# Input projection: two column halves in one matmul, drained by ACT and added by POOL

## The chip, the core and the metric

The kernel runs on one core of one Trainium2 chip, in one launch. The metric is device time in microseconds, the median of several executions. TensorE (PE in the profile) multiplies matrices into PSUM; VectorE (DVE), ScalarE (ACT) and GpSimd (POOL) work element by element; SyncE (SP) issues the transfers.

## The reference

Two layers over a sequence of 512 positions with 2048 features, in float32. The change concerns the first projection of the first layer alone:

```python
h = rmsnorm(x, norm_g)
proj = h @ w_in                       # 512 x 2048 times 2048 x 8192
u, gate = proj[..., :W_A], proj[..., W_A:]
u = u.reshape(B, S, N_POOL_GROUPS, G_A)
pooled = jnp.stack([causal_mean_pool(u[:, :, gi], w) - u[:, :, gi]
                    for gi, w in enumerate(POOL_WINDOWS)], axis=2)
y = jnp.einsum('bsgc,gcd->bsgd', pooled, w_group).reshape(B, S, W_A) * scale
return x + (y * jax.nn.silu(gate)) @ w_out
```

The second layer (latent attention) follows. It is not touched.

## The kernel before, in words

**High and low parts.** Every float32 operand is held as two fp32r numbers, a high part and the remainder. A product is three matmuls: high weights by high x, high weights by low x, low weights by high x.

**Seven products.** The projection's 64 output tiles (128 features by 512 positions) are computed as 32 pairs. For the last 30 pairs a 2 x 2 scheme with seven products in place of eight is used: the two output tiles of the pair, the two contraction tiles `2j`, `2j+1` and the two halves of the positions (`H` = 256 columns) form 2 x 2 blocks. `w_combos` (L300) loads 2 x 256 KB of weights for a quarter `q` of the contraction (two values of j), forms the sums of weights that the scheme needs (DVE L308, POOL L310 and L311), casts all seven to high parts (ACT L314) and subtracts for the low parts (DVE L315). Raw weights have three buffers, high and low weights two each. The sums of x are made once, ahead (`x_parts`, `x_sums`), into `xcp[j]`, a tile of 128 x (2, 7, 256): high and low, seven products, 256 columns.

**Matmuls.** `seven` (L326) is called for each j. For each of the seven products it issues three 256-column matmuls (L333, L335, L337) into one half of a PSUM bank. A pair has eight j (`NJ`), so 8 x 7 x 3 = 168 matmuls, and the text calls a quarter of it (42) a step. A pair's four banks hold the seven products; pairs alternate between two sets of four banks. Several products of the scheme go to both output tiles, so `gather` (L340) combines the products: one ACT copy of a half bank (L343), then four DVE additions that each read one input from PSUM (L344 to L347). The two results go to DRAM (L356), or, for the first four pairs of the u features (pairs 0 to 3, late in the loop), first through `pool_tile` (L235), which runs on DVE (L243, L250, L256, L259) with a small POOL memset.

**Around it.** Before the loop, four gate tiles are accumulated for all j into four banks `accs` while x is prepared (L386 to L388, with 256 and 512 columns mixed), copied out by ACT (L396) and stored. In the loop, the sum of squares of x is formed in the pairs n = 1 to 8 (`squares`: ACT L408, DVE L410), and n = 9 makes the norm from it (`norm_r`, with `rsqrt` at L156). The stages after the loop use 512-column matmuls (L144 to L146).

**Order.** The order of each engine's instructions is settled when the program is built: a list scheduler walks the traced instructions with a simulated timeline and fixes a list for every engine, and on the chip each engine works its list in order, waiting on semaphores. A tile pool with `bufs` buffers makes the writer of a buffer wait for the readers of its former content.

Of the kernel before, what the change touches and what calls it, by code (L numbers as in the profile page):

```python
# [14 lines left out]
P = 128  # L15
# [32 lines left out]
def trunk_kernel(  # L48
# [213 lines left out]
    with ExitStack() as c1:  # L262
# [4 lines left out]
        ps7 = [c1.enter_context(tc.tile_pool(name=f"ps7{i}", bufs=1, space=bass.MemoryType.PSUM, **tile_))  # L267
               for i in range(2)]
        xh, xl = [None] * NJ, [None] * NJ
# [7 lines left out]
        def x_parts(j, c, hp):  # L277
# [4 lines left out]
            xh[j], xl[j] = h, lo  # L282
# [37 lines left out]
        def banks(n):  # L320
            return [ps7[n % 2].tile([P, 2, H], F32, tag=f"k{i}", name=f"k{i}") for i in range(4)]


        SEVEN = ((2, 0, 0, 0), (0, 6, 1, 0), (1, 2, 2, 0), (3, 4, 3, 0),
                 (5, 5, 0, 1), (6, 1, 1, 1), (4, 3, 2, 1))

        def seven(ks, w, j):
            hi, lo = w
            for wi, xi, b, h in SEVEN:
                dst = ks[b][:, h, :]  # L330
                first, last = j == 0 and h == 0, j == NJ - 1

                T.matmul(dst, hi[:, j % 2, wi, :], xh[j][:, xi, :], start=first, stop=False,  # L333
                         skip_group_check=True)
                T.matmul(dst, hi[:, j % 2, wi, :], xl[j][:, xi, :], start=False, stop=False,  # L335
                         skip_group_check=True)
                T.matmul(dst, lo[:, j % 2, wi, :], xh[j][:, xi, :], start=False, stop=last,  # L337
                         skip_group_check=True)

        def gather(ks, pair):  # L340

            e = epool.tile([P, 7, H], F32, tag="e", name="e")
            A.copy(e[:, 6, :], ks[2][:, 0, :])  # L343
            V.tensor_tensor(e[:, 0:2, :], e[:, 6:7, :].broadcast_to([P, 2, H]), ks[0], ALU.add)  # L344
# [14 lines left out]
        accs = banks(1)  # L359
# [801 lines left out]
```

## Time and profile before

| what | value |
|---|---|
| median of 3 runs | 1923.71 us (1923.11 to 1924.19) |
| span of the profiled execution | 1921.5 us |
| median less span | 2.2 us |
| granted TensorE clock | 1.000 |
| input projection with seven products, first to last matmul | 52.7 to 661.4 us |
| PE, DVE, ACT, POOL busy in the whole span | 99%, 67%, 42%, 15% |

The profile shows one execution: for each engine the instructions with start and duration, grouped by line of the code and by the names of output and inputs. A bracket or the field behind the last bar gives the idle time before an instruction and who ended it. The record of a matmul lasts longer than its share of the engine, since matmuls overlap, so the pace is read from the starts. An instruction's record on DVE or POOL includes time in which it was held up after its start. Only the span of the profiled execution is known, and the 2.2 us around it come from the median.

### The profile page before, as it was taken

The page shows a single profiled execution, that of the slowest core. Times are in us where ns is not written, and L with a number is a line of the kernel's source. Part 1 is how long each engine was busy: PE and PEld are TensorE (multiplying, and loading weights), DVE is VectorE, ACT ScalarE, POOL GpSimd, SP SyncE. Part 2 cuts the span into 40 slices and gives each one's busy share as a digit, 9 for nine tenths or more (in the row PEclk, how much of TensorE's full clock was granted, in tenths as well). Part 3 has the DMA queues.
Part 4 walks back from the last instruction along what each step waited for, and adds up shares of the span by engine and source line. Part 5 has one row for each costly group of instructions (what it writes and reads, how often), then busy time and mean ns, then how long its engine had stood idle before and what let it go on. Part 6 is the DMA issues. An engine that isn't in the chain of part 4 may idle for free.

```text
span 1921.5 us, 30674 instructions
## 1 busy us (share of the span) xinstructions
PE 1906.1 (99%) x11356; PEld 1704.7 (89%) x11356; DVE 1278.6 (67%) x2252; ACT 807.1 (42%) x1509; POOL 280.9 (15%) x436
## 2 busy tenths in 40 slices
PE   8999999999999999999999999999999999999999
PEld 7999999999999988888888888888888898988887
DVE  8677785797666777496595476564325888897332
ACT  8443433333333433233333355233225777775221
POOL 0333233343222100000000000000001232320000
PEclk9999999999999999999999999999999999999999
DMA  6454444344444546344334344333333222234632
GB/s 191 155 164 157 151 132 133 121 131 135 147 146 135 159 154 214 119 128 142 119 123 137 110 146 134 89 98 120 121 121 90 87 90 69 85 124 144 203 116 88
DMA packets 177078, 251.26 MB, mean 131 GB/s; under 512 B 15776, under 2 KB 96800, under 8 KB 176928
## 3 DMA queue, kind: packets, MB, share of 16 engines
q1 hardware_dynamic: 176640, 249.10, 41.4%
q8 instruction: 89, 1.46, 0.3%
q14 instruction: 61, 0.50, 0.1%
q10 hardware_dynamic: 288, 0.20, 0.0%
HBM read 216.21 MB, written 33.03 MB: 130 GB/s over the span
## 4 chain that ended last, share of the span: by engine, by line
PE 94%; DVE 3%; DMA 1%; issue 1%; ACT 0%; SPq 0%; POOL 0%; DVEq 0%; POOLq 0%; ACTq 0%
PE mm L145 16%; PE mm L146 16%; PE mm L144 16%; PE k L337 10%; PE k L335 10%; PE k L333 10%; PE sc L786 3%; PE mm L641 2%; PE mm L643 2%; PE mm L642 2%; PE mm L664 1%; PE mm L666 1%; PE mm L665 1%; PE tr L814 1%; PE tr L752 1%; DMA raw<-awin 1%
## 5 line engine op out<-in xcount | busy, mean ns | idle before, releaser
L126 ACT CAST whi<-raw 128x512 fp32r<-128x512 f32 (+2 forms) x424 | 255.9, 607 | 518.6 <-PE mm L145 438.5
L333 PE MATMUL k<-xc,hi 128*128 128x256 f32 x1680 | 460.1, 283 | 0.0
L335 PE MATMUL k<-xc,hi 128*128 128x256 f32 x1680 | 460.0, 283 | 0.0
L127 DVE TENSOR_TENSOR wlo<-raw,whi 128x512 fp32r<-128x512 f32 (+2 forms) x424 | 285.7, 675 | 235.7 <-ACT whi L126 232.6
L337 PE MATMUL k<-xc,lo 128*128 128x256 f32 x1680 | 417.9, 283 | 2.2 <-DVE lo L315 2.2
L146 PE MATMUL mm<-bt,wlo 128*128 128x512 f32 x944 | 368.1, 390 | 0.0
L144 PE MATMUL mm<-bt,whi 128*128 128x512 f32 x944 | 367.7, 390 | 0.0
L145 PE MATMUL mm<-bt,whi 128*128 128x512 f32 x944 | 367.2, 389 | 0.0
L314 ACT CAST hi<-raw 128x1792 fp32r<-128x1792 f32 x120 | 202.8, 1690 | 364.9 <-PE k L337 249.6
L315 DVE TENSOR_TENSOR lo<-raw,hi 128x1792 fp32r<-128x1792 f32 x120 | 246.7, 2056 | 159.7 <-ACT hi L314 159.6
L333 PEld LDWEIGHTS k<-xc,hi 128*128 128x128 f32 x1680 | 322.5, 192 | 0.2 <-ACT hi L314 0.2
L335 PEld LDWEIGHTS k<-xc,hi 128*128 128x128 f32 x1680 | 322.5, 192 | 0.0
L337 PEld LDWEIGHTS k<-xc,lo 128*128 128x128 f32 x1680 | 296.8, 192 | 3.3 <-DVE lo L315 2.8
L146 PEld LDWEIGHTS mm<-bt,wlo 128*128 128x128 f32 x944 | 177.2, 188 | 37.5 <-DVE wlo L127 0.5
L144 PEld LDWEIGHTS mm<-bt,whi 128*128 128x128 f32 x944 | 177.2, 188 | 36.9 <-ACT whi L126 0.2
L145 PEld LDWEIGHTS mm<-bt,whi 128*128 128x128 f32 x944 | 177.3, 188 | 36.8
L145 PE MATMUL mm<-at,whi 128*128 128x512 f32 x432 | 169.0, 391 | 1.0 <-DVE at L149 1.0
L144 PE MATMUL mm<-at,whi 128*128 128x512 f32 x432 | 168.8, 391 | 0.0
L146 PE MATMUL mm<-at,wlo 128*128 128x512 f32 x432 | 168.2, 389 | 0.0
L310 POOL TENSOR_TENSOR raw<-raw 128x256 f32<-128x256 f32 x120 | 98.6, 821 | 439.9 <-DVE raw L308 422.1
L311 POOL TENSOR_TENSOR raw<-raw 128x256 f32<-128x256 f32 x120 | 99.1, 826 | 9.2
L145 PEld LDWEIGHTS mm<-at,whi 128*128 128x128 f32 x432 | 81.1, 188 | 19.2 <-DVE at L149 2.6
(1151 smaller groups left out, 2541.0 us busy)
## 6 DMA issues: line engine op xcount, KB each, us to landing
raw<-awin SPq DMA_DIRECT2D x240, 256.0 KB, 3.2
raw<-awo SPq DMA_DIRECT2D x128, 256.0 KB, 2.9
raw<-bwin SPq DMA_DIRECT2D x80, 256.0 KB, 2.8
raw<-awg SPq DMA_DIRECT2D x64, 256.0 KB, 2.8
scr<-e SPq DMA_DIRECT2D x56, 256.0 KB, 2.6
raw<-bwo SPq DMA_DIRECT2D x56, 256.0 KB, 2.9
raw<-wkvb SPq DMA_DIRECT2D x32, 256.0 KB, 3.0
raw<-wqb SPq DMA_DIRECT2D x32, 192.0 KB, 2.4
```

Of the source, the lines that this page charges most:

```text
L126: A.copy(hi[:, :n], raw[:, :n])
L127: V.tensor_tensor(lo[:, :n], raw[:, :n], f(hi[:, :n]), ALU.subtract)
L144: T.matmul(dst, wh, xh, start=first, stop=False)
L145: T.matmul(dst, wh, xl, start=False, stop=False)
L146: T.matmul(dst, wl, xh, start=False, stop=last)
L310: G.tensor_tensor(c[:, :, 6, :], c[:, :, 4, :], c[:, :, 2, :], ALU.add)
L311: G.tensor_tensor(c[:, :, 7, :], c[:, :, 6, :], c[:, :, 3, :], ALU.add)
L314: A.copy(hi, c[:, :, 1:8, :])
L315: V.tensor_tensor(lo, c[:, :, 1:8, :], f(hi), ALU.subtract)
L333: T.matmul(dst, hi[:, j % 2, wi, :], xh[j][:, xi, :], start=first, stop=False, skip_group_check=True)
L335: T.matmul(dst, hi[:, j % 2, wi, :], xl[j][:, xi, :], start=False, stop=False, skip_group_check=True)
L337: T.matmul(dst, lo[:, j % 2, wi, :], xh[j][:, xi, :], start=False, stop=last, skip_group_check=True)
```

## The change

High weights are applied to high and low x in one matmul of 512 columns: the moving operand is `xhl[j][:, :, xi, :]`, two stretches of 256 columns from the tile that holds both. Its output fills a whole bank, high by high in the first half and high by low in the second. The low weights by high x are added to the second half by a 256-column matmul. A product therefore takes a whole bank, and a pair seven banks out of a ring of eight. In a step, the work goes product by product with both values of j for each, in place of j by j.

At the pair's end, ACT copies each of the seven banks to SBUF (tile `d`, three buffers), POOL adds the two halves of each into the tile `e`, and DVE's four additions then read `e` alone. The pool for `e` has one buffer in place of two and eight slots of 256 columns in place of seven; `squares` gets a tile of its own, and the four gate tiles are copied out through `d`.

```diff
-        def seven(ks, w, j):
+        SEVEN = ((1, 2, 5), (2, 0, 0), (5, 5, 1), (4, 3, 2), (3, 4, 6), (0, 6, 3), (6, 1, 4))
+
+        def seven(ks, w, q):
             hi, lo = w
-            for wi, xi, b, h in SEVEN:
-                dst = ks[b][:, h, :]
-                first, last = j == 0 and h == 0, j == NJ - 1
-                T.matmul(dst, hi[:, j % 2, wi, :], xh[j][:, xi, :], start=first, stop=False,
-                         skip_group_check=True)
-                T.matmul(dst, hi[:, j % 2, wi, :], xl[j][:, xi, :], start=False, stop=False,
-                         skip_group_check=True)
-                T.matmul(dst, lo[:, j % 2, wi, :], xh[j][:, xi, :], start=False, stop=last,
-                         skip_group_check=True)
+            for i, (wi, xi, _) in enumerate(SEVEN):
+                for j in (2 * q, 2 * q + 1):
+                    T.matmul(ks[i], hi[:, j % 2, wi, :], xhl[j][:, :, xi, :], start=j == 0, stop=False,
+                             skip_group_check=True)
+                    T.matmul(ks[i][:, 1, :], lo[:, j % 2, wi, :], xh[j][:, xi, :], start=False,
+                             stop=j == NJ - 1, skip_group_check=True)
 
         def gather(ks, pair):
-            e = epool.tile([P, 7, H], F32, tag="e", name="e")
-            A.copy(e[:, 6, :], ks[2][:, 0, :])
-            V.tensor_tensor(e[:, 0:2, :], e[:, 6:7, :].broadcast_to([P, 2, H]), ks[0], ALU.add)
-            V.tensor_tensor(e[:, 2, :], e[:, 1, :], ks[2][:, 1, :], ALU.add)
-            V.tensor_tensor(e[:, 3:6:2, :], e[:, 1:3, :], ks[3][:, 0:1, :].broadcast_to([P, 2, H]), ALU.add)
-            V.tensor_tensor(e[:, 4:7:2, :], e[:, 2:4, :], ks[1], ALU.add)
-            for i, v in enumerate((e[:, 0:7:6, :], e[:, 4:6, :])):
+            e = epool.tile([P, 8, H], F32, tag="e", name="e")
+            for k, (_, _, i) in zip(ks, SEVEN):
+                d = dpart.tile([P, 2, H], F32, tag="d", name="d")
+                A.copy(d, k)
+                G.tensor_tensor(e[:, i, :], d[:, 0, :], d[:, 1, :], ALU.add)
+            V.tensor_tensor(e[:, 0:2, :], e[:, 5:6, :].broadcast_to([P, 2, H]), e[:, 0:2, :], ALU.add)
+            V.tensor_tensor(e[:, 2, :], e[:, 1, :], e[:, 2, :], ALU.add)
+            V.tensor_tensor(e[:, 5:8:2, :], e[:, 1:3, :], e[:, 6:7, :].broadcast_to([P, 2, H]), ALU.add)
+            V.tensor_tensor(e[:, 3:5, :], e[:, 2:6:3, :], e[:, 3:5, :], ALU.add)
+            for i, v in enumerate((e[:, 0:5:4, :], e[:, 3:8:4, :])):
...
-        epool = c1.enter_context(tc.tile_pool(name="epool", bufs=2, **tile_))
+        epool = c1.enter_context(tc.tile_pool(name="epool", bufs=1, **tile_))
+        dpart = c1.enter_context(tc.tile_pool(name="dpart", bufs=3, **tile_))
...
-            ks = banks(n)
+            ks = [bank() for _ in range(7)]
             for q in range(NJ // 2):
-                w = w_combos(pair, q)
-                seven(ks, w, 2 * q)
-                seven(ks, w, 2 * q + 1)
+                seven(ks, w_combos(pair, q), q)
```

Here `bank()` takes the next of eight one-bank PSUM tiles (`ps7.tile([P, 2, H], F32, tag="k", name="k")`), and the norm at n = 9 takes one of them too.

More of the change, by code (lines that the diff above doesn't have):

```diff
@@ L265, in trunk_kernel @@
         w7 = c1.enter_context(tc.tile_pool(name="w7", bufs=2, **tile_))
-        ps7 = [c1.enter_context(tc.tile_pool(name=f"ps7{i}", bufs=1, space=bass.MemoryType.PSUM, **tile_))
-               for i in range(2)]
-        xh, xl = [None] * NJ, [None] * NJ
+        ps7 = c1.enter_context(tc.tile_pool(name="ps7", bufs=8, space=bass.MemoryType.PSUM, **tile_))
+        xh, xl, xhl = [None] * NJ, [None] * NJ, [None] * NJ
         def x_load(j):
@@ L356, in gather @@
                     nc.sync.dma_start(raws[o].rearrange("p (h t) -> p h t", h=2), v)
-        accs = banks(1)
+        accs = [bank() for _ in range(4)]
         with ExitStack() as c2:
```

25 lines of the change are left out of this document (10 added, 15 removed).

## The prediction

> **What bounds the kernel now.** I read the busy times first, then the costliest groups, then the input projection by windows and instruction by instruction.
>
> ```profile
> span 1921.5 us, 30674 instructions
> PE 1906.1 (99%) x11356; PEld 1704.7 (89%) x11356; DVE 1278.6 (67%) x2252; ACT 807.1 (42%) x1509; POOL 280.9 (15%) x436
> L337 PE MATMUL k<-xc,lo 128*128 128x256 f32 x1680 | 417.9, 283 | 2.2 <-DVE lo L315 2.2
> L314 ACT CAST hi<-raw 128x1792 fp32r<-128x1792 f32 x120 | 202.8, 1690 | 364.9 <-PE k L337 249.6
> ```
>
> TensorE is busy 99% of the span. In the projection it was kept waiting 2.2 us in all (by the low weights, L315), while ACT's weight cast waits for TensorE. So the projection is bound by TensorE, and by its pace, not by a wait. The windows (busy us and instruction counts of PE, PEld, DVE, ACT, POOL, then clock, DMA share, GB/s) show a plain stretch and the busiest one, where pooling runs beside it:
>
> ```profile
> 420.00:440.00 20.00, 20.00 (x169) 20.00 (x168) 19.48 (x21) 6.90 (x5) 9.52 (x10) 1.00 0.43 132
> 560.00:580.00 20.00, 20.00 (x169) 20.00 (x169) 12.66 (x13) 7.03 (x5) 5.91 (x8) 1.00 0.47 145
> ```
>
> DVE is the second engine. Now one step (a quarter of a pair: 42 matmuls, one weight cast, one low part), on ACT, DVE and POOL, at a pair's end:
>
> ```profile
> 540.81 1.69 ACT L314 CAST hi<-raw 128x1792 fp32r<-128x1792 f32 x1 [3.35 <-PE k L337]
> 545.85 1.70 ACT L314 CAST hi<-raw 128x1792 fp32r<-128x1792 f32 x1 [3.08 <-issue]
> 542.53 2.02 DVE L315 TENSOR_TENSOR lo<-raw,hi 128x1792 fp32r<-128x1792 f32 x1 [2.41 <-ACT hi L314]
> 544.47 0.69 DVE L308 TENSOR_TENSOR raw<-raw 128x512 f32<-128x512 f32 x1
> 545.29 0.74 POOL L310 TENSOR_TENSOR raw<-raw 128x256 f32<-128x256 f32 x1 [3.49 <-DVE raw L308]
> 546.11 0.74 POOL L311 TENSOR_TENSOR raw<-raw 128x256 f32<-128x256 f32 x1
> ```
>
> The casts start 545.85 - 540.81 = 5.04 us apart: 5.04/42 = 0.120 us a 256-column matmul, 20.16 us a pair (four steps), 604.8 us for 30. A step's chain is cast then low part: 542.53 + 2.02 = 544.55, which is 1.3 us before the next step.
>
> **The change, part by part.** (1) TensorE. The pace of 512 columns is read in a later stage, that of a mixture of widths from the gate columns before the projection (32 times six of 256 and three of 512):
>
> ```profile
> 1349.64 0.39 PE L145 MATMUL mm<-bt,whi 128*128 128x512 f32 x1
> 1355.99 0.39 PE L146 MATMUL mm<-bt,wlo 128*128 128x512 f32 x1
> 35.81 0.28 PE L386 MATMUL k<-xc,hi 128*128 128x256 f32 x1
> 41.43 0.28 PE L386 MATMUL k<-xc,hi 128*128 128x256 f32 x1
> ```
>
> Twenty-eight starts lie between the first two: 6.35/28 = 0.2268 us. Four groups of nine lie between the last two: 5.62/4 = 1.405 us, against 6 x 0.120 + 3 x 0.2268 = 1.400; changing widths costs between nothing and 0.0025 us a change. A product of one j was 3 x 0.120 = 0.360 and becomes 0.2268 + 0.120 = 0.3468: 13.2 ns less, 1680 times 22.2 us. With two width changes each the gain would be 22.2 - 1680 x 0.005 = 13.8; I take 22.2, since 0.005 in nine starts is about what stamps of 0.01 leave open. A pair needs 56 x 0.3468 = 19.42 us of TensorE.
>
> The Trainium skill ("TensorE: Matmul & The Clock Gate", Back-to-back issue gap) has matmuls follow each other at N/2.4 + 2.5 ns, so merging two would save 2.5 ns, an estimate of 4.2 us in all; the trace has a fixed part of 13 ns (0.120 twice against 0.2268), and the measurement decides.
>
> (2) ACT drops one 256-column copy a pair (L343) and drains seven whole banks. The nearest rows are four such copies:
>
> ```profile
> 51.71 2.04 ACT L396 COPY e<-k 128x512 f32<-128x512 f32 x4
> ```
>
> 2.04/4 = 0.51, so 3.6 us a pair beside four casts of 1.69: 10.4 us of 19.4. ACT has room; queued behind a drain is the next cast, which may be 3 us late before TensorE lacks high weights (1.69 of 5.04 used). That cover ends if drains wait.
>
> (3) POOL gets seven adds of 128x256 a pair beside its eight (L310, L311): same operation, shape and type, 0.74 each, 5.2 us more, 11.1 us of 19.4. (4) DVE's four gather operations stay, but now all their inputs lie in SBUF; before, each read PSUM. On busy time alone nothing here reaches 19.4 us. But POOL and DVE get in each other's way, and this decides. First a low part and a POOL add that starts inside it, then the reverse, then the pooling stretch, where they alternate, then a gather operation that reads PSUM:
>
> ```profile
> 58.67 2.02 DVE L315 TENSOR_TENSOR lo<-raw,hi 128x1792 fp32r<-128x1792 f32 x1
> 58.89 2.39 POOL L310 TENSOR_TENSOR raw<-raw 128x256 f32<-128x256 f32 x1 [2.83 <-DVE raw L308]
> 63.64 0.74 POOL L311 TENSOR_TENSOR raw<-raw 128x256 f32<-128x256 f32 x1
> 63.84 2.42 DVE L315 TENSOR_TENSOR lo<-raw,hi 128x1792 fp32r<-128x1792 f32 x1 [1.16 <-ACT hi L314]
> ...
> 399.69 1.70 ACT L314 CAST hi<-raw 128x1792 fp32r<-128x1792 f32 x1 [3.34 <-PE k L337]
> ...
> 409.46 0.69 DVE L243 SCALAR_TENSOR_TENSOR tt__4532<-e,r 128x512 f32<-128x512 f32 x1
> 409.68 1.06 POOL L310 TENSOR_TENSOR raw<-raw 128x256 f32<-128x256 f32 x1 [3.47 <-DVE raw L308]
> 410.18 1.12 DVE L250 TENSOR_TENSOR tt__4535<-tt__4532 128x512 f32<-128x512 f32 x1
> 410.82 1.07 POOL L311 TENSOR_TENSOR raw<-raw 128x256 f32<-128x256 f32 x1
> 411.50 2.27 DVE L315 TENSOR_TENSOR lo<-raw,hi 128x1792 fp32r<-128x1792 f32 x1 [0.20 <-ACT hi L314]
> 414.97 1.23 DVE L243 SCALAR_TENSOR_TENSOR tt__4542<-e,r 128x512 f32<-128x512 f32 x1
> ...
> 565.23 0.68 DVE L344 TENSOR_TENSOR e<-e,k 128x512 f32<-128x512 f32 x1
> 565.45 0.73 POOL L310 TENSOR_TENSOR raw<-raw 128x256 f32<-128x256 f32 x1 [3.48 <-DVE raw L308]
> ```
>
> The add at 58.89 ends at 61.28, 0.59 after the low part's end (60.69). In the alternation each ends a fixed time after the other: L243 at 410.15, L310 at 410.74 (+0.59), L250 at 411.30 (+0.56), L311 at 411.89 (+0.59), L315 at 413.77 (+1.88). So two such operations exclude each other, with holds of 0.59 (POOL, 256), 0.56 (DVE, 512) and 1.88 (DVE, 1792). The gather operation with a PSUM input overlaps the add, and neither is longer. Call the time in which either holds this path shared time.
>
> Shared time a pair before: DVE 4 x (1.88 + 0.56) = 9.76, POOL 8 x 0.59 = 4.72: 14.48 of 20.16. After: seven adds 7 x 0.59 = 4.13, and gather 3 x 0.56 + 0.28 = 1.96 (it loses its PSUM input): 20.57, against TensorE's 19.42. Beside this run, as before, fourteen additions of squares (L410), ten operations of the norm (one addition, L161 to L163) and six a pair of pooling in four pairs (two each of L243, L250, L259), 48 x 0.56 = 26.9. The stage needs 30 x 20.57 + 26.9 = 644.0 us of shared time; TensorE 582.6. What is late next is the cast, through L310 and L311 queued behind the adds on POOL, and the low part.
>
> How well is it used? In four pooling pairs of the old kernel it was 14.48 + 6 x 0.56 = 17.84 of 20.16, 88%, and TensorE never stopped, so 88% is a floor for what it can reach. At 100% the stage is 644.0 - 604.8 = 39 us longer; at 88%, 644.0/0.88 = 732, 127 us longer. The seven adds are ready only as banks finish and may wait through the next pair (the banks themselves need three buffers and six drains by the next pair's first step), so much of the idle can be filled; I take 98%: 657.1, or +52.
>
> The hold of the new adds isn't shown itself. From below, it is DVE's for as many elements, 0.28: then 20.57 - 7 x 0.31 = 18.4 a pair, and TensorE stays the bound. From above, the record's 0.74: 21.6 a pair, 675.5 in all, +71. I take 0.59, the row of the same operation and shape.
>
> The Trainium skill ("SBUF — State Buffer", Who interferes with whom) says that a VectorE operation with two SBUF inputs and a reading GpSimd operation hold a shared port for the whole instruction and the other blocks. The trace agrees on who blocks. Taken with whole records it makes 4 x 2.71 + 3.5 x 0.69 + 15 x 0.74 = 24.4 us a pair, an estimate near +160; the rows in alternation are shorter, and they decide.
>
> (5) Small: one e buffer in place of two, freed by its store, is wanted a pair later: nothing, except in the four pooling pairs, whose second L243 reads it until 414.97 + 1.23 = 416.2. The pair's end was the step at 399.69, the next pair's last step starts at 399.69 + 3 x 5.04 = 414.8, and its first add comes some 2 us later: it is met if pooling runs late by more than a microsecond, 0 to 4 us in all. Last pair's banks drain while the next stage starts, and j = 6 is released only with j = 7: 0 to 3 us. I add 1. DMAs: none added; stores on SP's queue keep their place.
>
> **Sum.** Profiled span 1921.5, and 2.2 around it to the median of 1923.7. 1921.5 + 52 + 1 + 2.2 = 1976.7, say 1977.
>
> **Rivals.** *TensorE stays the bound* (faster): the new adds hold the path for 0.42 us or less: without them a pair's shared time is 20.57 - 4.13 = 16.44, and 7 of them must fit into 19.42 - 16.44 = 2.98. For it: POOL is 15% busy, DVE 67%, and the four pairs at 88% ran without a stop. Against: the operation is L310's. Then 1923.7 - 22.2 + 1 = 1902. Chance 0.12. *About no change*: buffers smooth a hold just under 0.59, or the shorter matmuls just pay for it: 1920 to 1928, chance 0.06. *A bad order on top* (slower still): drains and adds stand ahead of the cast and of L310/L311 in the fixed orders, so each pair's second and third casts are late by more than their 3 us; 1.5 us a pair beyond the forecast, +45: 2022. For it: POOL and ACT run strictly in order. Against: the next cast is only delayed by one drain if the order is by readiness. Chance 0.17. *Whole-record holds*: 1923.7 + 160 = 2084; the ends in alternation speak against it, chance 0.03. *The merge saves nothing* (a moving operand in two stretches runs at 0.240): shared time still decides, so the time is the forecast's; it only matters in the first rival. The forecast itself (shared time is the bound, 95 to 100% of it used: 644/0.95 = 678, +73, so 1964 to 1998, and 1960 to 2005 with the open ends of parts 1 and 5) has 0.62.
>
> **How the numbers follow.** What a measurement can tell from no change is 0.2%, 3.9 us. Faster 0.12, same 0.06, slower 0.62 + 0.17 + 0.03 = 0.82. The range runs from the no-change case to between the bad order and whole records, 1920 to 2045, leaving 0.12 below and about 0.05 above; the forecast's own range is 1960 to 2005.
>
> **What would show it.** In the changed kernel's trace: starts 0.2268 and 0.120 apart where TensorE runs freely (part 1); adds (L310's kind, POOL) with mean records over 1 us, and low parts well above 2.03 mean (shared time); TensorE idle before the low matmul or the first high one, released by L315 or L314, some 74 us in all (657 - 583); POOL and DVE ends alternating at 0.59 and 0.56. It is wrong if TensorE stays above 98% busy in the projection, if adds beside low parts keep 0.74, or if the idle is released by the drains (banks) and not by the weights.

## The result, and the profile after

| | before | after |
|---|---|---|
| median | 1923.95 us (1923.11 to 1926.33, 4 runs) | 2034.11 us (2032.21 to 2035.19, 4 runs) |
| ratio, 95% interval | | 1.0572 (1.0559 to 1.0584): slower |
| span of the profiled execution | 1921.5 us | 2030.4 us |
| projection with seven products, first high matmul of the first pair to the last low one | 609.0 us | 709.8 us |
| TensorE idle in it, before its matmuls | 2.2 us | 80.4 us |

The change costs 110 us where the prediction had 53. Of the span's 108.9 us, 100.8 lie in the projection itself.

The page of the changed kernel: busy time of each engine, the chain that ended last, then the costliest groups (busy us, mean ns of one, idle time before them and what ended it). The high matmul is now L329, the low one L331, the weight sums L309 and L310, the cast L313, the low part L314, the adds L340.

```profile
span 2030.4 us, 27822 instructions
PE 1931.0 (95%) x9676; PEld 1632.3 (80%) x9676; DVE 1404.4 (69%) x2252; ACT 907.8 (45%) x1689; POOL 661.9 (33%) x646
...
PE 71%; POOL 10%; DVE 9%; DMA 5%; issue 3%; ACT 1%; SPq 1%; DVEq 0%; POOLq 0%; ACTq 0%
...
L329 PE MATMUL k<-xc,hi 128*128 128x512 f32 x1680 | 559.9, 403 | 5.0 <-ACT hi L313 2.8
L331 PE MATMUL k<-xc,lo 128*128 128x256 f32 x1680 | 387.8, 293 | 75.4 <-DVE lo L314 75.3
...
L314 DVE TENSOR_TENSOR lo<-raw,hi 128x1792 fp32r<-128x1792 f32 x120 | 274.2, 2300 | 28.0 <-ACT hi L313 27.9
L340 POOL TENSOR_TENSOR e<-d 128x256 f32<-128x256 f32 x210 | 209.0, 1017 | 23.0 <-ACT d L339 23.0
L310 POOL TENSOR_TENSOR raw<-raw 128x256 f32<-128x256 f32 x120 | 213.4, 1778 | 6.8
L309 POOL TENSOR_TENSOR raw<-raw 128x256 f32<-128x256 f32 x120 | 162.5, 1354 | 157.6 <-DVE raw L307 125.2
```

TensorE stops for the low part, L314, almost alone. An add's record means 1.02 us, the weight sums have grown from 0.82 to 1.35 and 1.78, the low part from 2.06 to 2.30. The three groups on POOL make 585 us, most of the stage, but these records hold time in which POOL is held up.

The waits of the changed kernel (engine, line, whom it waits for; us in all, times, longest):

```profile
ACT hi L313 <- POOL raw L310: 156.4, 59, 4.8
...
DVE e L341 <- POOL e L340: 54.9, 29, 6.6
ACT d L339 <- POOL e L340: 53.5, 42, 3.6
DVE raw L307 <- DMA raw<-awin: 52.1, 35, 3.4
```

The first number also held time in which nothing was urgent (the cast waited 249.6 us for TensorE before). The second and third are new: VectorE's gather and ScalarE's drains wait for POOL's adds. What that does is seen at a pair's end, instruction by instruction (start, duration, engine, operation, and in brackets the idle time before it with its releaser): DVE, then ACT, POOL and PE.

```profile
627.67 1.21 DVE L341 TENSOR_TENSOR e<-e 128x512 f32<-128x512 f32 x1 [2.03 <-POOL e L340]
628.98 0.78 DVE L342 TENSOR_TENSOR e<-e 128x256 f32<-128x256 f32 x1
629.69 2.56 DVE L314 TENSOR_TENSOR lo<-raw,hi 128x1792 fp32r<-128x1792 f32 x1
632.17 1.22 DVE L307 TENSOR_TENSOR raw<-raw 128x512 f32<-128x512 f32 x1
633.31 1.23 DVE L343 TENSOR_TENSOR e<-e 128x512 f32<-128x512 f32 x1
635.17 1.22 DVE L344 TENSOR_TENSOR e<-e 128x512 f32<-128x512 f32 x1 [0.63 <-POOL e L340]
636.54 1.00 DVE L307 TENSOR_TENSOR raw<-raw 128x512 f32<-128x512 f32 x1 [0.16 <-DMA raw<-awin]
...
632.87 1.70 ACT L313 CAST hi<-raw 128x1792 fp32r<-128x1792 f32 x1 [2.76 <-POOL raw L310]
...
630.32 2.52 POOL L310 TENSOR_TENSOR raw<-raw 128x256 f32<-128x256 f32 x1
632.80 2.33 POOL L340 TENSOR_TENSOR e<-d 128x256 f32<-128x256 f32 x2
...
639.52 0.39 PE L331 MATMUL k<-xc,lo 128*128 128x256 f32 x1 [2.03 <-DVE lo L314]
```

The cast that starts at 632.87 ends at 634.57. Its low part could start there, but on DVE's list L344 and L307 stand ahead of it, and L344 waits for an add. It starts behind L307, at about 637.5, some 2.9 us late, and TensorE stands still for 2.03 us. Of the 2.9 us, 0.60 is the wait for the add. Most of the rest are the two records, 1.22 and 1.00 us; 128 x 512 took DVE 0.69 in the prediction's rows where nothing held it up, so being held up beside POOL lengthens the delay as well.

Read in this manner, the 57 stops of the stage divide as follows, by the instruction directly ahead of the late low part or cast. 26 of them, 47.0 us, are low parts behind the weight sum L307 on DVE, and in 20 of these L344 stands ahead of L307, as in the rows above. 14 stops, 7.8 us, are low parts behind the gather's L342; four, 14.4 us, stand behind pooling's L250. The rest is at most 2.8 us a cause (drains ahead of the cast: 2.2 us).

The stage then adds up. At the prediction's pace its matmuls need 30 x 19.42 = 582.6 us. Stops add 80.4. The granted clock fell below 0.95 in 18 of the stage's windows of 5 us, and the sum of (1 - clock) x 5 us is 25.5 us; it was 0 before. At each of the 57 stops the last matmul's record runs on beyond its slot (0.39 against 0.2268, 0.28 against 0.120, so 0.16): 9.3 us more. Together 697.8 of 709.8. The remaining 12 is nearly what the kernel without adds, below, has too (10.4). Behind the stage 7.6 us more pass to the end than before, of which the kernel without adds has 4.3 too; their cause is open.

### The profile page after: what moved, and what is told of

Its sections match the earlier page's. It is cut to its first block, busy times and chain, and to the rows that moved or that the text cites. A ratio compares the mean times of both kernels' runs of the same rounds, so it can differ in the third digit from the quotient of the medians.

```text
span 2030.4 us, 27822 instructions
## 1 busy us (share of the span) xinstructions
PE 1931.0 (95%) x9676; PEld 1632.3 (80%) x9676; DVE 1404.4 (69%) x2252; ACT 907.8 (45%) x1689; POOL 661.9 (33%) x646
## 4 chain that ended last, share of the span: by engine, by line
PE 71%; POOL 10%; DVE 9%; DMA 5%; issue 3%; ACT 1%; SPq 1%; DVEq 0%; POOLq 0%; ACTq 0%
PE mm L145 15%; PE mm L146 15%; PE mm L144 15%; PE k L329 6%; POOL e L340 5%; DVE lo L314 5%; PE k L331 4%; DMA raw<-awin 3%; POOL raw L310 3%; PE sc L779 2%; POOL raw L309 2%; PE mm L634 2%; PE mm L636 1%; PE mm L635 1%; PE mm L657 1%
## 5 line engine op out<-in xcount | busy, mean ns | idle before, releaser
L329 PE MATMUL k<-xc,hi 128*128 128x512 f32 x1680 | 559.9, 403 | 5.0 <-ACT hi L313 2.8
L331 PE MATMUL k<-xc,lo 128*128 128x256 f32 x1680 | 387.8, 293 | 75.4 <-DVE lo L314 75.3
L127 DVE TENSOR_TENSOR wlo<-raw,whi 128x512 fp32r<-128x512 f32 (+2 forms) x424 | 285.2, 674 | 238.5 <-ACT whi L126 235.7
L331 PEld LDWEIGHTS k<-xc,lo 128*128 128x128 f32 x1680 | 332.5, 198 | 131.8 <-DVE lo L314 96.5
L329 PEld LDWEIGHTS k<-xc,hi 128*128 128x128 f32 x1680 | 315.9, 193 | 47.0 <-ACT hi L313 5.1
L313 ACT CAST hi<-raw 128x1792 fp32r<-128x1792 f32 x120 | 203.4, 1695 | 306.3 <-POOL raw L310 156.4
L314 DVE TENSOR_TENSOR lo<-raw,hi 128x1792 fp32r<-128x1792 f32 x120 | 274.2, 2300 | 28.0 <-ACT hi L313 27.9
L340 POOL TENSOR_TENSOR e<-d 128x256 f32<-128x256 f32 x210 | 209.0, 1017 | 23.0 <-ACT d L339 23.0
L310 POOL TENSOR_TENSOR raw<-raw 128x256 f32<-128x256 f32 x120 | 213.4, 1778 | 6.8
L309 POOL TENSOR_TENSOR raw<-raw 128x256 f32<-128x256 f32 x120 | 162.5, 1354 | 157.6 <-DVE raw L307 125.2
L307 DVE TENSOR_TENSOR raw<-raw 128x512 f32<-128x512 f32 x120 | 119.3, 994 | 52.5 <-DMA raw<-awin 52.1
```

Of the source, the lines that this page charges most:

```text
L127: V.tensor_tensor(lo[:, :n], raw[:, :n], f(hi[:, :n]), ALU.subtract)
L309: G.tensor_tensor(c[:, :, 6, :], c[:, :, 4, :], c[:, :, 2, :], ALU.add)
L310: G.tensor_tensor(c[:, :, 7, :], c[:, :, 6, :], c[:, :, 3, :], ALU.add)
L313: A.copy(hi, c[:, :, 1:8, :])
L314: V.tensor_tensor(lo, c[:, :, 1:8, :], f(hi), ALU.subtract)
L329: T.matmul(ks[i], hi[:, j % 2, wi, :], xhl[j][:, :, xi, :], start=j == 0, stop=False, skip_group_check=True)
```

## The experiments

In the tables, "stage" and "idle" are measured as above. All kernels ran beside the kernel before, whose median was between 1922.3 and 1924.2. An interval is given where the kernel ran more than once. Theory A in the expectations is the prediction's, the sum of shared time; theory E is formed on the way and told where it is tested.

### What each part is worth: no adds, or adds in the old kernel

`no_adds` is the change without POOL's adds. Only the first half of each bank is copied to `e`, so the second halves (low weights, and high by low) are missing from its result.

```diff
-                A.copy(d, k)
-                G.tensor_tensor(e[:, i, :], d[:, 0, :], d[:, 1, :], ALU.add)
+                A.copy(e[:, i, :], k[:, 0, :])
```

> The changed kernel without POOL's seven adds: ACT copies the first half of each bank into e, and the second halves (high weights by low x, low weights by high x) are left out of the sums. Theory A: as with the adds on DVE, 1903 to 1912, and the low parts' mean record falls from 2.30 back to about 2.05. Theory B: the drains remain, but no d buffer waits for POOL; banks and e are as before, so some 1950 or more.

`before_7` and `before_14` leave the old kernel as it is, with 7 or 14 POOL adds of the same shape behind the gather of each pair; nobody reads what they write.

```diff
+            for i in range(7):
+                u = upool.tile([P, H], F32, tag="u", name="u")
+                G.tensor_tensor(u, e[:, 4 + i % 2, :], e[:, 6, :], ALU.add)
```

> The kernel before with 7 more POOL additions of 128x256 a pair after its gather (14 made it 2075). Theory A: shared time 14.48 + 7 x 0.59 = 18.6 us a pair, 92% of 20.16, which is what the run with 14 adds reached, so hardly any stop: 1924 to 1945. Theory E: POOL's seven adds stand together before the next sums of weights, 4 to 7 us in a row, longer than the slack of a step, and TensorE stops once a pair: 1960 or more.

> The kernel before (256-column matmuls, four banks, its own gather) with 14 more POOL additions of 128x256 a pair, which read the gathered e and write a scratch tile that nobody reads. Theory A: shared time 14.48 + 14 x 0.59 = 22.74 us a pair, with the side work 709 us: at full use the time is 2028, at the 91% of the changed kernel 2098. Theory B: banks, d and the merged matmuls aren't there, so the time stays within 10 us of 1924.

| kernel | time, us | ratio | stage | idle |
|---|---|---|---|---|
| no_adds | 1918.66 | one run | 598.6 | 5.6 |
| before_7 | 1988.84 | 1.0343 (1.0322 to 1.0363) | 670.5 | 41.3 |
| before_14 | 2075.39 | one run | 755.3 | 96.7 |

The first and the fifth of five casts in a row of `no_adds`, so one pair:

```profile
545.28 1.69 ACT L313 CAST hi<-raw 128x1792 fp32r<-128x1792 f32 x1 [3.19 <-PE k L331]
...
564.83 1.69 ACT L313 CAST hi<-raw 128x1792 fp32r<-128x1792 f32 x1 [3.19 <-PE k L331]
```

A pair takes 564.83 - 545.28 = 19.55 us, against 20.16 before and 19.42 predicted: the merge is worth 0.61 us a pair (predicted 0.74), and TensorE is the bound again, here with 5.6 us of stops in the stage. The stage is 10.4 us shorter than before (its first three pairs take 21.4, 22.2 and 21.5 us), and 5 us are left over the whole kernel, in one run. Theory A expected 1903 to 1912, so 7 to 16 us less; theory B's 1950 is refuted. The adds, with the larger drains and the `d` buffers, cost the other 115 us.

Seven adds cost 66 us in the old kernel as well, where the banks are drained as ever and nobody waits for their result. Theory E expected 1960 or more there, theory A at most 1945. They reach TensorE mainly through POOL's list: 22.1 of the 40.2 us of stops, 30 of 49, hang on weight sums behind L350. POOL and ACT of `before_7`:

```profile
603.32 7.86 POOL L350 TENSOR_TENSOR u<-e 128x256 f32<-128x256 f32 x5 [0.94 <-DVE e L347]
611.14 0.73 POOL L310 TENSOR_TENSOR raw<-raw 128x256 f32<-128x256 f32 x1
...
613.98 1.70 ACT L314 CAST hi<-raw 128x1792 fp32r<-128x1792 f32 x1 [6.63 <-POOL raw L311]
```

Five adds take 7.86 us beside DVE's work, the weight sums stand behind them, and the cast waits 6.63 us. Fourteen adds cost 152 us, more than double: of the stops there, 68.5 us in 64 stops hang on casts that wait for weight sums behind L350.

### Is the sum of shared time the bound?

Two kernels take work out of that sum. `dve_adds` copies one half by ACT and lets DVE add the other half from PSUM. DVE's additions with an input in PSUM ran beside POOL's undisturbed in the old kernel (L344 in the prediction), so a pair's sum goes back to 20.57 - 4.13 = 16.4 us. `wsum_dve` gives the weight sums to DVE: eight holds of 0.59 become eight of 0.28, and the sum is 18.1.

```diff
-                A.copy(d, k)
-                G.tensor_tensor(e[:, i, :], d[:, 0, :], d[:, 1, :], ALU.add)
+                A.copy(d[:, 0, :], k[:, 1, :])
+                V.tensor_tensor(e[:, i, :], k[:, 0, :], d[:, 0, :], ALU.add)
```

> The changed kernel, but ACT copies only the second half of each bank and DVE adds the first half straight from PSUM; POOL adds nothing. Theory A (POOL and DVE exclude each other, shared time is the bound): shared time a pair falls from 20.57 to 16.44 us, 85% of TensorE's 19.42, below the 88% that the pooling pairs of the old kernel bore; TensorE is the bound again, the stage shrinks from 710 to about 585 us, the time is 1903 to 1915. Theory B (the way through seven banks, three d buffers and one e buffer is what holds TensorE): the same banks are drained one by one through the same buffers, so most of the loss stays, over 1990. Theory C (DVE's own busy time is the bound): 7 more additions, 2.9 us a pair, so at least as slow, over 2034.

```diff
-            G.tensor_tensor(c[:, :, 6, :], c[:, :, 4, :], c[:, :, 2, :], ALU.add)
-            G.tensor_tensor(c[:, :, 7, :], c[:, :, 6, :], c[:, :, 3, :], ALU.add)
+            V.tensor_tensor(c[:, :, 6, :], c[:, :, 4, :], c[:, :, 2, :], ALU.add)
+            V.tensor_tensor(c[:, :, 7, :], c[:, :, 6, :], c[:, :, 3, :], ALU.add)
```

> The changed kernel with the two sums of weights (L309, L310) on DVE in place of POOL; POOL keeps the seven adds alone, with three d buffers. Theory A: shared time 20.57 - 8 x (0.59 - 0.28) = 18.1 us a pair and no weight work stands behind the adds on POOL: 1908 to 1940. Theory B (drain chain through d and banks): the chain is unchanged, 2000 or more.

`memset` was to keep the chain from drain to gather, with POOL's part of it reading nothing: each add becomes one write over `d` and one over the slot of `e`, 0.84 us together. The products are missing from its result. The edit does more than its expectation says: the write over `e` no longer waits for a drain, and so the gather doesn't either.

```diff
-                G.tensor_tensor(e[:, i, :], d[:, 0, :], d[:, 1, :], ALU.add)
+                G.memset(d, 1.0)
+                G.memset(e[:, i, :], 1.0)
```

> The changed kernel with each POOL add replaced by two POOL memsets that read nothing: one over the drained d tile, one over the product's slot of e (so the products are left out of the result; the waits for ACT and for d and e stay). POOL's busy time stays of the same order. Theory A (adds and DVE exclude each other because both read SBUF): low parts' mean record back under 2.1 us, and 1908 to 1940. Theory B: the order, the chain and POOL's queue are the same, 2000 or more.

| kernel | time, us | ratio | stage | idle |
|---|---|---|---|---|
| dve_adds | 2017.22 | 1.0485 (1.0467 to 1.0502) | 697.0 | 75.5 |
| wsum_dve | 2033.74 | 1.0578 (1.0547 to 1.0609) | 713.0 | 93.4 |
| memset | 1982.66 | one run | 661.8 | 48.4 |

Theory A falls as the bound of these kernels. `wsum_dve` uses 18.1 of some 23.5 us a pair, 77%, and `dve_adds` 16.4 of 22.4, 73%; the old kernel did 88% without a stop. Both are about as slow as the change, which is what theory B expected (2000 or more, over 1990). Counted in the traces by records, POOL runs an addition or DVE an operation without a PSUM input in 85% of the stage of `wsum_dve` and 81% of that of `dve_adds`; in `no_adds`, with 5.6 us of stops, it is 92%, in the changed kernel 94%. In `wsum_dve` the low part's mean record is back at 2.04 us, as undisturbed as before, and yet TensorE waits longer for it. DVE and PE of `wsum_dve`:

```profile
608.16 0.69 DVE L307 TENSOR_TENSOR raw<-raw 128x512 f32<-128x512 f32 x1 [2.80 <-DMA raw<-awin]
608.77 2.02 DVE L314 TENSOR_TENSOR lo<-raw,hi 128x1792 fp32r<-128x1792 f32 x1
...
610.84 0.58 PE L331 MATMUL k<-xc,lo 128*128 128x256 f32 x1 [2.24 <-DVE lo L314]
```

DVE idles 2.80 us before L307, whose raw weights are late, with the low part next in its list. Nor is POOL itself the bound there: it has the adds alone, 210 of 1.12 us. In these rows, what stops TensorE is what stands at the head of a list, not how much an engine has to do. Another 31.9 us of stops (23) are low parts behind the gather's L343, in most of them with a weight sum, L310, further ahead: the edit also puts new work ahead of the low part.

`memset` can't tell the theories apart, and its 1982.66 lies outside both ranges. Its gather runs ahead of the matmuls, by 221 us in the last pair (first gather operation, last matmul):

```profile
494.70 0.69 DVE L342 TENSOR_TENSOR e<-e 128x512 f32<-128x512 f32 x1 [1.43 <-POOL e L341]
...
715.64 0.28 PE L331 MATMUL k<-xc,lo 128*128 128x256 f32 x1
```

So the first 20 pairs bear the work on `e` of all 30 and take 21 to 25 us each, and the nine full pairs behind them, without any of it, take 19.6 to 19.7. It is 64 us slower than `no_adds` and 51 faster than the change, and how much of either is order, sharing or load it doesn't show.

### Buffers and the order of the products

These undo or widen one thing each in the changed kernel: four buffers for raw weights, seven for `d`, three for high weights, and the former order, j by j. (Room for the buffers comes from three in place of six buffers for temporaries and from squaring x one tile at a time.)

```diff
-            c = w7.tile([P, 2, 8, P], F32, tag="raw", name="raw", bufs=3)
+            c = w7.tile([P, 2, 8, P], F32, tag="raw", name="raw", bufs=4)
```

> The changed kernel with four buffers of raw weights in place of three (to make room, three buffers of scratch in place of six, and the squares take one tile of x at a time). Shared time was used to 91% of the stage (644 of 710 us). Theory A1 (the missing 9% is L307 waiting 52 us for weights that arrive late because the raw buffer is freed late): use rises to 97%, the stage falls to about 664 us and the time to about 1990. Theory A2 (the missing share is the fixed order on POOL: L309 and L310 stand behind the adds, so the cast is late whatever is loaded): within 15 us of 2034.

```diff
-        dpart = c1.enter_context(tc.tile_pool(name="dpart", bufs=3, **tile_))
+        dpart = c1.enter_context(tc.tile_pool(name="dpart", bufs=7, **tile_))
```

> The changed kernel with seven d buffers in place of three (room made as before: three scratch buffers, squares by one tile of x), so that ACT can drain all seven banks of a pair without waiting for POOL. Theory A (POOL's adds are too many for the time that DVE leaves it, and everything behind them on POOL is late): within 20 us of 2034. Theory B (three d buffers hold the drains, the drains hold the banks, the banks hold TensorE): 1985 or less.

```diff
-            hi = w7.tile([P, 2, 7, P], F32R, tag="hi", name="hi")
+            hi = w7.tile([P, 2, 7, P], F32R, tag="hi", name="hi", bufs=3)
```

> The changed kernel with three buffers of high weights in place of two (room made with three scratch buffers and squares by one tile of x, which did not move the time beside four raw buffers). A cast may then run one step earlier, so the low part gains the cast's 1.7 us of lead. Theory A (the sum of what POOL and DVE hold exclusively is too long, throughput): the sums are the same, within 20 us of 2034. Theory E (the sums would fit, but cast and low part of single steps come 1.7 to 2.7 us late because their inputs stand behind adds, gather and loads in the fixed orders, latency): the stops shrink by about the lead, 1985 or less.

```diff
-            for i, (wi, xi, _) in enumerate(SEVEN):
-                for j in (2 * q, 2 * q + 1):
+            for j in (2 * q, 2 * q + 1):
+                for i, (wi, xi, _) in enumerate(SEVEN):
```

> The changed kernel with the former order of the work in a step: all seven products of one j, then of the next. All banks of a pair finish in the last half step, so the drains start some 2 us later and in a bunch. Theory A: the same work, within 20 us of 2034. Theory B/D (the moment at which banks come free sets TensorE's stops): 2060 or more.

| kernel | time, us | ratio | stage | idle |
|---|---|---|---|---|
| raw4 | 2034.89 | 1.0578 (1.0557 to 1.0599) | 708.7 | 79.1 |
| d7 | 2023.95 | one run | 695.6 | 71.8 |
| hi3 | 2074.20 | 1.0787 (1.0765 to 1.0808) | 741.0 | 99.4 |
| jbyj | 2034.29 | one run | 711.2 | 81.9 |

`raw4`, `d7` and `jbyj` stay within 20 us of the change, so none of these by itself is the cause; seven `d` buffers take away 10 us (one run), a third high buffer makes it 40 us worse, which no theory expected. The lists are fixed anew for each kernel by the list scheduler. In `d7`, 41.9 us of the stops are again low parts behind L307, but mostly with L341 and L342 ahead of it; in `hi3` it is 34.8 us, and 47.0 us more are waits for casts and drains, which were 5.0 in the changed kernel.

### Taking POOL out of the adds

`d7_dve` has seven `d` buffers and the adds on DVE, from SBUF. `e_direct` needs no `d`: ACT copies one half straight into `e`, and DVE adds the other from PSUM in place.

```diff
-                G.tensor_tensor(e[:, i, :], d[:, 0, :], d[:, 1, :], ALU.add)
+                V.tensor_tensor(e[:, i, :], d[:, 0, :], d[:, 1, :], ALU.add)
```

> As with seven d buffers, and DVE adds the halves from SBUF in place of POOL. Banks are freed by ACT alone. The run with adds from PSUM came to 2017; its trace suggests theory D: there a bank was free only after DVE's add, which stood behind low parts, and TensorE's fixed order then mixed two steps, so both buffers of high weights were held. Theory A with D: shared time 20.57 - 7 x (0.59 - 0.28) = 18.4 us a pair, below TensorE's 19.5; banks come free early; 1908 to 1935. Theory C (DVE's queue is the bound, whoever frees the banks): 2000 or more.

```diff
-                A.copy(d, k)
-                G.tensor_tensor(e[:, i, :], d[:, 0, :], d[:, 1, :], ALU.add)
+                A.copy(e[:, i, :], k[:, 0, :])
+                V.tensor_tensor(e[:, i, :], e[:, i, :], k[:, 1, :], ALU.add)
```

> The changed kernel without d and without POOL's adds: ACT copies the first half of a bank straight into e, DVE adds the second half from PSUM in place. Seven slots of e stand ready, so no drain waits for a buffer. Against the run with adds from PSUM through three d buffers (2017): theory B for that run (three d buffers hold the drains and so the banks) expects 1960 or less; theory D (banks come free only after a DVE operation that stands behind a low part, so TensorE's order mixes two steps) expects 2000 or more; theory A alone (shared time 16.4 us a pair) expects 1905 to 1920, which the earlier run already speaks against.

| kernel | time, us | ratio | stage | idle |
|---|---|---|---|---|
| d7_dve | 1966.12 | 1.0226 (1.0196 to 1.0256) | 640.4 | 34.7 |
| e_direct | 1953.30 | 1.0161 (1.0144 to 1.0178) | 632.1 | 23.3 |

Both are far shorter than the change, and still slower than the old kernel. `d7_dve` meets neither range of its expectation; `e_direct` meets theory B's, that three `d` buffers hold the drains. `e_direct` does the same work as `dve_adds` (seven half copies by ACT, seven additions on DVE with one PSUM input, 0.41 us each in both) and is 64 us faster. Its sum of shared time is the same 16.4 us, and DVE is busier in it (86% of the stage against 74%). What differs is the buffer that a copy needs: in `dve_adds` one of three `d`, which DVE's addition has to free (ACT's copies wait 82.5 us for those additions), in `e_direct` a slot of `e` (the additions are not among its main releasers). At equal work, what waits for what, and the lists made from it, is worth 64 us.

### Moving the gather out of the way

Theory E: DVE's four gather operations wait for POOL's adds and stand ahead of a low part; put them where the adds are long done, and the stops go. `late_gather` issues them behind the low part of the next pair's third step, `late_e_direct` does it in `e_direct`.

```diff
+        def combine(e, pair):
             V.tensor_tensor(e[:, 0:2, :], e[:, 5:6, :].broadcast_to([P, 2, H]), e[:, 0:2, :], ALU.add)
...
                 seven(ks, w_combos(pair, q), q)
+                if n and q == 2:
+                    with tc.issue_after(lows[-1]):
+                        combine(*held)
```

> The changed kernel, but the gather's four DVE operations (and what follows them, pooling and stores) are put behind the low part of the third step of the next pair; drains and POOL's adds stay where they are, and so do all sizes. Theory E (DVE works its list in order, and L341 and L342 wait there for POOL's adds with a ready low part behind them): the 45 us of stops behind L342 go, and with them part of the 25 us of lowered clock; 1960 to 1985. Theory A (shared time, 20.57 us a pair, is too long whatever the order): within 20 us of 2034.

> The run in which ACT copies a half into e and DVE adds the other from PSUM (1953), with the gather's four operations put behind the third step of the next pair as well. Only 5 us of its 26 us of stops stand behind gather or drains, 9 behind pooling: theory E expects 1935 to 1955. With the adds left out altogether the time was 1919, which is a floor for this. Against the kernel before (1923) no gain is expected.

In both the single `e` buffer was in the way: it is freed only when the moved gather's results are stored. So four kernels have two of them, with the gather in its old place or moved.

```diff
-            e = epool.tile([P, 8, H], F32, tag="e", name="e")
+            e = epool.tile([P, 8, H], F32, tag="e", name="e", bufs=2)
```

> The changed kernel with two e buffers and the gather where it is (room from 3 temporary buffers in place of 6 and squares loaded one x tile at a time). Theory E (DVE's gather operations wait for POOL's adds and stand ahead of the next low part; the single e buffer makes a later gather hold the adds and drains): the gather still stands ahead of the low part, so 2020 to 2036. Rival F (the single e buffer by itself is the delay): below 1990. Rival L (any edit only moves the stops through a new fixed order): 2015 to 2040.

> The same with the gather's four DVE operations put behind the low part of the next pair's third step. With one e buffer this was 2030.6, its adds and drains waiting for the e store. Theory E: both waits are gone, so at most 1985, TensorE idle in the stage under 40 us. Rival L: 2010 to 2040, idle over 60 us, the stops behind L310 on POOL or behind the cast. The sum of holds of the prediction: no operation is added or removed, so nothing changes: 2030.

> ACT copies one half of a bank into e, DVE adds the other half from PSUM in place, no POOL adds; now two e buffers. With one it was 1953.3 with 26.4 us of TensorE idle. Theory E: of that idle little hangs on the e buffer (5.7 us behind pooling's L243), so 1940 to 1954. Rival F: the buffer was most of it: 1925 to 1940.

> The same with the gather put behind the third low part of the next pair. With one e buffer it was 2008.7, TensorE waiting for drains that waited for the e store. Theory E: the buffer was that wait, so back to 1925 to 1955. Rival L: above 1985.

| kernel | time, us | ratio | stage | idle |
|---|---|---|---|---|
| late_gather | 2030.57 | 1.0552 (1.0535 to 1.0570) | 706.4 | 69.1 |
| late_e_direct | 2008.73 | 1.0441 (1.0426 to 1.0457) | 687.6 | 63.1 |
| after_e2 | 2039.60 | 1.0608 (1.0590 to 1.0626) | 711.3 | 80.5 |
| late_gather_e2 | 2023.37 | 1.0524 (1.0509 to 1.0540) | 695.2 | 75.9 |
| e_direct_e2 | 1951.08 | 1.0146 (1.0131 to 1.0161) | 630.7 | 22.2 |
| late_e_direct_e2 | 1963.51 | 1.0212 (1.0197 to 1.0227) | 641.9 | 35.5 |

Theory E falls too, as a whole. The expectation of `late_gather` counts 45 us of stops behind L342; they are 7.8 (above), and the 47.0 behind L307 have a gather operation ahead in 24 of 26 stops. Moving the gather did what it was to do on DVE: in `late_gather` TensorE waits 19.1 us for low parts, in place of 75.3. But now it waits 44.8 us for drains (2.2 in the changed kernel), which wait for adds and buffers, and the time stays in theory A's range. `late_e_direct` lies far above theory E's. With two `e` buffers, in `late_gather_e2`, only 1.9 us of stops are low parts directly behind a gather operation, and TensorE still stops for 75.9 us; it had to be at most 1985 us and is 2023. That is where the rival L had it, by which an edit only moves the stops; its range holds for `after_e2` too. With two `e` buffers, moving the gather saves 16 us (2039.6 to 2023.4), and in `e_direct_e2` it costs 12 (1951.1 to 1963.5, which meets neither range). Two things of theory E hold: `e_direct_e2` is in its range, and the second `e` buffer is worth 45 us to `late_e_direct`, so there the buffer was the wait. What takes the gather's place is seen in `late_gather_e2`, where 46.4 us are low parts behind L307, in a pattern that comes again in the plain pairs (stops at 605.88, 628.96, 651.41): ACT, DVE, SP and PE.

```profile
616.24 1.29 ACT L339 COPY d<-k 128x512 f32<-128x512 f32 x2 [3.11 <-POOL e L340]
617.42 1.69 ACT L313 CAST hi<-raw 128x1792 fp32r<-128x1792 f32 x1
...
619.20 2.35 DVE L314 TENSOR_TENSOR lo<-raw,hi 128x1792 fp32r<-128x1792 f32 x1 [3.58 <-ACT hi L313]
...
626.28 0.69 DVE L307 TENSOR_TENSOR raw<-raw 128x512 f32<-128x512 f32 x1 [3.58 <-DMA raw<-awin]
626.89 2.02 DVE L314 TENSOR_TENSOR lo<-raw,hi 128x1792 fp32r<-128x1792 f32 x1
...
621.58 0.88 SPq L303 DMA_DIRECT2D raw<-awin  x2
...
628.96 0.39 PE L331 MATMUL k<-xc,lo 128*128 128x256 f32 x1 [2.18 <-DVE lo L314]
```

A drain waits 3.11 us for an add to free a `d` buffer. The cast behind it in ACT's list is late; the low part, which waits 3.58 us for that cast, ends at 621.55 and only then frees its raw buffer; the load that wants the buffer is issued at 621.58; L307 waits for it at the head of DVE's list and starts 4.7 us later; the low part behind L307 is late, and TensorE stops for 2.18 us. Every link is a wait for something that finished late, and DVE, ACT and POOL each idle for several us in the same pair.

Left open: which list would have no such link, and how much of the loss is the lateness of the adds and how much the time for which DVE and POOL hold each other up. The combination of moved gather, two `e` and seven `d` buffers was not tried. Since every edit has its lists fixed anew, the single waits can't be priced one by one, and the 64 us between `dve_adds` and `e_direct` is the nearest to a price that these runs give.

## Why the prediction was wrong, point by point

**Part 1, TensorE: right.** 0.2268 and 0.120 hold wherever TensorE runs freely at full clock: in the changed kernel, L329, then two L331, then the next L329 come 0.47 us apart (639.75, 640.21, 640.68). A pair takes 19.55 us without adds, 0.13 over the sum; 30 pairs at 0.61 are 18.3 us, of the 22.2 predicted. The formula of the Trainium skill ("TensorE: Matmul & The Clock Gate", Back-to-back issue gap), which that section gives for an isolated matmul, would by the prediction's estimate have made the merge worth 4.2 us; the measurement is nearer to the fixed part of 13 ns, as said.

**Part 2, ACT has room: right in time, wrong in consequence.** ACT is busy 45% and its drains ahead of the cast cause only 2.2 us of the stops. But drains wait for adds (53.5 us), and after other waits are removed this one passes on to the cast (`late_gather_e2`).

**Parts 3 and 4, POOL and DVE: the records right, the bound wrong.** The adds' mean is 1.02 us (said: over 1), low parts 2.30 (said: well above 2.03), TensorE's idle 80.4 us (said: some 74), released by L314. Ends alternate as well: L314 at 632.25, L310 at 632.84 (+0.59), L307 at 633.39 (+0.55). These signs of shared time all came, and DVE and POOL do hold each other up, but the sum doesn't set the end of the stage: the failing step is "the stage needs 30 x 20.57 + 26.9 = 644.0 us of shared time" taken as what sets the end, and with it "I take 98%"; 644.0 is 91% of the measured 709.8. Kernels with 16.4 and 18.1 us of it a pair stop about as long (75.5 and 93.4 us), where it had TensorE as the bound. What the traces show in its place: the adds, slowed by DVE, finish late, and lists that run in order wait behind them. That this is how the 115 us arise is read from the rows; no run has removed the waits and kept the adds' load. The sum came near the idle time by luck, by its size and not by its reason.

**The term that was missing.** The forecast's stage grows by 52.3: 74.5 idle less 22.2. Measured are 100.8: 78.2 more of idle less the same 22.2, and with it 25.5 us of lost clock, 9 of records at stops, 10 of other parts (8 of which the kernel without adds has too). So the idle time was 4 us off, and what stops do to the matmuls around them, 35 us (lost clock and longer records), was put at nothing. The 7.6 us behind the stage, against 1 for part 5, make up most of what is left.

**Part 5: right on the buffer, too small in all.** A second `e` buffer in the changed kernel gains nothing (2039.6 against 2034.1). Pooling was priced at 0 to 4 us, as a late reader of `e`; it costs 14.4 us of stops another way, with low parts behind L250 on DVE's list.

**The rivals.** *TensorE stays the bound* failed in the adds, not in the pace: `no_adds` is that case with 1918.7, not 1902. *A bad order on top*, 2022, names the mechanism that the runs support, lists whose heads wait, and is nearest in time. It had the wrong list: the casts and weight sums were to stand behind drains and adds, as they do in `before_14`; in the changed kernel it is the low part behind the weight sum and the gather. It was costed as an extra on top of a full resource, and its nearness in time is luck too. *Whole-record holds*, 2084, isn't reached, but since no sum of holds is the bound, the time doesn't test them. *The merge saves nothing* is refuted by the 19.55 us.

## What to carry to other kernels

When work moves to an engine with time to spare, add up not only its busy time but each wait in the lists: what stands behind an instruction that now waits for a slower producer, and whose buffer that frees. A chain of copy, add and gather across three engines was enough to stop TensorE once or more in every pair, though none of them was busy for the whole stage (POOL 81%, DVE 78%, ACT 45%). And where TensorE starts to stop for 2 us or more at a time, add the lost clock to the price of the stop, here a third of it again. In `dve_adds`, 75.5 us in 92 stops, 3 of them over 2 us against 21 here, cost 6.8 us of clock.

## What the hardware showed unexpectedly

**The clock falls after short stops, sometimes.** TensorE of the changed kernel after a stop of 2.04 us, and after one of 3.76:

```profile
234.81 0.39 PE L331 MATMUL k<-xc,lo 128*128 128x256 f32 x1 [2.04 <-DVE lo L314]
...
235.74 0.60 PE L331 MATMUL k<-xc,lo 128*128 128x256 f32 x2
236.14 0.63 PE L329 MATMUL k<-xc,hi 128*128 128x512 f32 x1
236.57 0.63 PE L331 MATMUL k<-xc,lo 128*128 128x256 f32 x2
236.99 0.63 PE L329 MATMUL k<-xc,hi 128*128 128x512 f32 x1
...
239.39 0.39 PE L329 MATMUL k<-xc,hi 128*128 128x512 f32 x1
...
424.44 0.58 PE L331 MATMUL k<-xc,lo 128*128 128x256 f32 x1 [3.76 <-DVE lo L314]
...
429.94 0.58 PE L329 MATMUL k<-xc,hi 128*128 128x512 f32 x1
430.35 0.28 PE L331 MATMUL k<-xc,lo 128*128 128x256 f32 x1
```

From 235.7 to 239.2, 3.4 us, the step from one L329 to the next is 0.85 us in place of 0.47: half speed, and it begins 0.9 us after TensorE has resumed. The stop of 2.03 us at 639.52 has no such stretch behind it. After 3.76 us, half speed is there at once and lasts 5.9 us. The windows (busy us of PE, PEld, DVE, ACT, POOL, granted clock, DMA share, GB/s) say the same of the three:

```profile
235.00:240.00 5.00, 5.00 (x23) 4.44 (x23) 2.93 (x2) 0.14 (x1) 3.08 (x3) 0.66 0.59 170
425.00:430.00 5.00, 5.00 (x20) 4.42 (x19) 4.95 (x7) 0.00 (x0) 0.43 (x2) 0.50 0.60 176
640.00:645.00 5.00, 5.00 (x30) 4.38 (x29) 2.85 (x3) 1.70 (x1) 3.04 (x3) 1.00 0.60 184
```

The Trainium skill ("TensorE: Matmul & The Clock Gate", Part 1: The HAM clock gate) has the clock at half after an idle window of about 3.4 us, until a busy window has passed, with windows that run freely. The length of 3.4 us and the half agree, and that one stop of 2 us is followed by it and the next isn't fits windows that run freely; that a stop of 2.04 us can be enough, the trace adds.

**POOL can be shut out for several operations of DVE.** The prediction had them take turns. `d7_dve`, POOL and then DVE:

```profile
617.12 6.21 POOL L309 TENSOR_TENSOR raw<-raw 128x256 f32<-128x256 f32 x1 [2.63 <-DVE raw L307]
...
616.91 2.01 DVE L314 TENSOR_TENSOR lo<-raw,hi 128x1792 fp32r<-128x1792 f32 x1
618.85 0.41 DVE L342 TENSOR_TENSOR e<-e 128x256 f32<-128x256 f32 x1
619.18 0.41 DVE L340 TENSOR_TENSOR e<-d 128x256 f32<-128x256 f32 x1
619.52 0.68 DVE L343 TENSOR_TENSOR e<-e 128x512 f32<-128x512 f32 x1
620.12 2.02 DVE L314 TENSOR_TENSOR lo<-raw,hi 128x1792 fp32r<-128x1792 f32 x1
622.06 0.68 DVE L344 TENSOR_TENSOR e<-e 128x512 f32<-128x512 f32 x1
```

DVE runs six operations with two SBUF inputs without a gap, none of them longer than when it is alone, and POOL's one add of 0.74 us ends 0.59 after the last (622.74 + 0.59 = 623.33). So POOL isn't let in between them here; in the prediction's rows it was, at each end. What tells the two cases apart these runs don't show.
